# Statistics queued later, the last combinations, a chunk's split and the first stores placed anew in a float32 encoder layer

## The chip, the core and the metric

The kernel runs on one core of one Trainium2 chip. Its time is the device time of one execution in microseconds (us), given as a median of several executions. Beside it stands one profiled execution, from which all durations come. The engines are called as the profile calls them: PE is TensorE (matrix products), PEld its weight loads, DVE is VectorE, ACT is ScalarE, POOL is GpSimd, SP is the engine that issues most transfers. Each takes its instructions in the order in which they were queued.

## The reference, cut to what matters

One layer over 512 tokens of width 2048, all in float32:

```python
xn = rms_norm(x, attn_norm_g)
u_val, u_gate, q, k, v = split(xn @ w_in)
y_conv = conformer_conv(u_val, u_gate, ...)       # GLU, depthwise conv of 31, layer_norm, silu
y_na = neighborhood_attention(q, k, v, rpb)       # 16 heads of 64 on an 8 x 64 grid
mixed = concat([rms_norm(y_conv, conv_out_g), rms_norm(y_na, na_out_g)])
x = x + mixed @ w_out
xn = rms_norm(x, ffn_norm_g)
gate, val = split(depthwise_conv(xn @ w_up, width=3))
x = x + (silu(gate) * val) @ w_down
return rms_norm(x, final_norm_g)
```

`w_up` has 2 x 5632 columns, `w_down` 5632 rows. Every norm needs a sum over all channels of a token before anything can be scaled by it.

## The kernel before, in words

**Layout.** Activations lie with channels on the 128 partitions and the 512 tokens along the free axis. A float32 product is made of three passes in a faster format: weights and activations are split into a high part (rounded, a ScalarE copy, `whi`, line 116) and the rest (a VectorE subtraction, `wlo`, line 117), and `mm3` (lines 127 to 129) adds high x high, high x low and low x high. A unit of weights is 128 x 1024; there are four buffers of each part (`NW`) and seven of raw loads (`NR`), and SP loads a unit when its raw buffer is free.

**Order of work.** The program is written as one stream, and a scheduler orders each engine's queue by priorities (the place in the source, moved by `shifted`) and by what is ready in its own model. Statistics and attention are generators whose steps are queued between the matrix products: `tick` (called when a group of products has been issued) takes the next step from `steps` and from `asteps`. A `yield` in a generator thus means "the rest later, behind the next group of products". A `yield` more or less moves all that follows by one group.

**Statistics of group A.** `group_a` (lines 367 to 396) sums the eight convolution outputs on VectorE (line 373), sums over the partitions by a product with ones (line 376), subtracts the mean, sums the squares (`sum_sq`, line 170), and calls `rsqrt_steps` twice. `rsqrt_steps` sums over partitions to one value per token (line 185), takes the reciprocal root on four values per partition (`root`, lines 173 to 177), spreads it over a diagonal (`dg`, line 197), and yields; its rest multiplies ones with the two diagonals (line 202) and copies the result out (line 206). Both its products use the bank "po" of the pool `psa`. Attention runs beside this: a softmax on VectorE and ScalarE (its last step line 466), transposes on TensorE (line 476), values (line 491), and products that read and write the same pools.

**Output projection and the combinations.** `after` (called for each of 16 blocks d) adds the projection to the residual (line 595), stores it, queues its square for a sum in memory, and on every second block combines two blocks of activations into seven (`b`, `t`, `xc`; lines 609 to 620, `halves` at lines 589 and 590). These seven are the moving side of the up product: the 2 x 2 blocks of weights (A11 to A22) and activations are multiplied with seven products instead of eight. The weights' combinations (lines 650 to 661, on VectorE) are in `factors`.

**The up and down products.** For each of 44 columns f, seven products are made, each over eight k. For the first four columns `up_apart` (line 755) makes them with `mm3`; later `up` (line 669) makes a wide pass (line 700, 512 columns) and a narrow one (line 705, 256 columns). Products use three banks "mm" in turn; the seventh uses "po". ScalarE and VectorE copy and add them out (lines 712 to 751 and 771 to 779), scale by `rstd2` (lines 794, 795), convolve (786 to 788), apply silu (797) and multiply (798). `stats2` loads the sums of squares and makes `rstd2` with `rsqrt_steps`. Four columns f make a chunk; `in_two` splits each column's result (`hh` on ScalarE, line 803, `hl` on VectorE, line 804), and the chunk's down products are issued within the next chunk (`down`, `down_units`).

**The end.** The last chunk's down products are made for 384 tokens (channels on partitions) and 128 tokens (tokens on partitions). `finish` scales a pair of blocks for the 384 tokens, on VectorE, or with ScalarE and GpSimd together for every third pair, and stores it (line 877, `out_T`); `spread` places this between the last products. The 128 tokens are scaled by gains (line 920) and by their own factor (lines 929, 931) and stored in four parts (line 932, `out_N`).

Of the kernel before, what the change touches and what calls it, by code (L numbers as in the profile page):

```python
# [10 lines left out]
F32 = mybir.dt.float32  # L11
# [5 lines left out]
P = 128  # L17
D = 2048
# [33 lines left out]
ORDER = "aavaav" + "aq" * 4 + "qqqq"  # L52
NORM_AT = 4
NG = GW // 8
RA_AFTER = 5

PCOLS = [("g1", KD), ("dww", NC_ * CK), ("dwb", NC_), ("lng", NC_), ("lnb", NC_), ("cog", NC_),
         ("nag", NC_), ("g2", KD), ("fww", 2 * NF * 3), ("fwb", 2 * NF), ("g3", KD)]
# [9 lines left out]
def layer(ctx: ExitStack, tc: tile.TileContext, xT, xG, w_in, w_v, w_out, w_up, w_down, par, tab, g3, out, last_out):  # L68
# [17 lines left out]
    def t2(name, dt=F32):  # L86
        return tp.tile([P, S], dt, tag="t2k", name=name)
# [76 lines left out]
    def sum_sq(acc, src, first, to=slice(0, S)):  # L164
        if first:
            nc.scalar.activation(acc, src, AF.Square)
        else:
            q = t2("sq")[:, to]
            nc.scalar.activation(q, src, AF.Square)
            nc.vector.tensor_add(acc, acc, q)  # L170
# [5 lines left out]
        nc.vector.tensor_mul(y, y, v)  # L176
        nc.vector.scalar_tensor_tensor(y, y, 1.5, r, op0=ALU.add, op1=ALU.mult)

    def rsqrt_steps(acc, n, name, to=slice(0, S), keep=True, by_token=None):

        m = (to.stop - to.start) // P
        ps = psa.tile([P, S], F32, tag="po", name="st")[:, :m]
        v, r, y = (sm.tile([P, S // P], F32, tag="rs" + c, name="rs" + c)[:, :m] for c in "vry")
        for i in range(m):
            nc.tensor.matmul(ps[:, i:i + 1], acc[:, to.start + i * P:to.start + (i + 1) * P], ones[:, 0:1],
                             start=True, stop=True)
        nc.vector.tensor_scalar(v, ps, 1.0 / n, EPS, op0=ALU.mult, op1=ALU.add)
        root(r, y, v)
        if by_token is not None:
            by_token.append(y)  # L190
        yh, yl = (sm.tile([P, S // P], dt, tag="rs" + c, name="rs" + c)[:, :m] for c, dt in (("h", F32R), ("l", F32)))
        nc.vector.tensor_copy(yh, y)
        nc.vector.tensor_sub(yl, y, yh.bitcast(F32))
        ds = []
        for part in (yh.bitcast(F32), yl):
            ds.append(t2("dg", F32R)[:, :m * P])
            nc.vector.tensor_mul(ds[-1].rearrange("p (i k) -> p i k", k=P), ident.unsqueeze(1).broadcast_to([P, m, P]),
                                 part.unsqueeze(2).broadcast_to([P, m, P]))
        yield
        ps = psa.tile([P, S], F32, tag="po", name="st")[:, :m * P]  # L200
        for i, dg in enumerate(ds):
            nc.tensor.matmul(ps, ones_r, dg, start=i == 0, stop=i == 1)
        if not keep:
            return ps
        res = t2(name)
        nc.scalar.activation(res, ps, AF.Copy)
        return res
# [157 lines left out]
    ma, ra = [], []  # L365

    def group_a():
        yield
        yield
        acc = t2("acc")  # L370
        nc.vector.tensor_add(acc, ys[0], ys[1])
        for i in range(2, NC_):
            nc.vector.tensor_add(acc, acc, ys[i])
        yield
        ps = psa.tile([P, S], F32, tag="po", name="st")
        nc.tensor.matmul(ps, ones, acc, start=True, stop=True)
        mu = t2("mu")
        nc.vector.tensor_scalar(mu, ps, 1.0 / CONV, None, op0=ALU.mult)
        acc = t2("acc")
        for i in range(NC_):  # L380
            nc.vector.tensor_sub(ys[i], ys[i], mu)
            sum_sq(acc, ys[i], i == 0)
        yield
        yield
        r = yield from rsqrt_steps(acc, CONV, "rln")
        acc = t2("acc")
        for i in range(NC_):
            nc.vector.tensor_mul(ys[i], ys[i], r)
            nc.scalar.activation(ys[i], ys[i], AF.Silu, scale=pc("lng", i), bias=pc("lnb", i))
            ma.append(split(ys[i], pc("cog", i), "ma"))  # L390
        for i in range(NC_):
            sum_sq(acc, ys[i], i == 0)
        for _ in range(RA_AFTER):
            yield

        ra.append((yield from rsqrt_steps(acc, CONV, "ra")))


# [194 lines left out]
    def after(d, ps):  # L593

        nc.vector.tensor_add(x2[d], x2[d], ps)
        nc.sync.dma_start(xd[d], x2[d])
        q = t2("sq")
        nc.scalar.activation(q, x2[d], AF.Square)

        if d < 2:  # L600
            nc.gpsimd.dma_start(sq2[d], q)
        else:
            nc.gpsimd.dma_start(sq2[d % 2], q, accum_op=ALU.add)
        if d % 2 == 0:
            return
        b = []
        for i in (d - 1, d):
            t = t2("b")
            nc.scalar.activation(t, x2[i], AF.Copy, scale=pc("g2", i))
            b += [t[:, :H], t[:, H:]]  # L610
        b11, b12, b21, b22 = b
        t = t2("t")
        t1, t2_ = t[:, :H], t[:, H:]
        nc.vector.tensor_sub(t1, b11, b12)
        nc.vector.scalar_tensor_tensor(t2_, b22, -1.0, t1, op0=ALU.mult, op1=ALU.subtract)
        t = t2("t")
        t3, t4_ = t[:, :H], t[:, H:]
        nc.vector.tensor_sub(t3, b22, b12)
        nc.vector.scalar_tensor_tensor(t4_, t2_, -1.0, b21, op0=ALU.mult, op1=ALU.subtract)
        for c, f in enumerate((t4_, t1, t3, b11, t2_, b21, b22)):  # L620
            halves(f, c)
# [9 lines left out]
    def stats2():  # L631
        acc2, q = t2("acc2"), t2("sq")
        nc.sync.dma_start(acc2, sq2[0])
        nc.sync.dma_start(q, sq2[1])
        yield
        nc.vector.tensor_add(acc2, acc2, q)
        rstd2.append((yield from rsqrt_steps(acc2, D, "rstd2")))

    def factors(f):

# [113 lines left out]

    def up_apart(f, between):

        def product(c):
            w = weights()
            ps = (psa.tile([P, S], F32, tag="po", name="pu") if c == 6 else
                  psm.tile([P, S], F32, tag="mm", name="pu"))[:, :H]  # L760
            for k in range(U):
                m = comb[c][k]
                i = mm3(ps, w, k, m[:, :H], m[:, H:], k == 0, k == U - 1)
            tick(i)
            between(c)
            return ps

        vv, v, uu, g = (t2(n).rearrange("p (i t) -> p i t", i=2) for n in ("vv", "vl", "uu", "g"))
        both = lambda x: x.unsqueeze(1).broadcast_to([P, 2, H])
        for i in range(2):  # L770
            nc.scalar.activation(vv[:, i], product(i), AF.Copy)
        u, u2 = uu[:, 0], uu[:, 1]
        add(v, vv, both(product(2)))
        nc.scalar.activation(u, product(3), AF.Copy)
        add(u2, u, product(4))
        add(v, v, both(u2))
        add(vv[:, 1], vv[:, 1], u2)
        add(g[:, 0], u, product(5))
        add(g[:, 1], vv[:, 1], product(6))
        return tuple(t.rearrange("p i t -> p (i t)") for t in (g, v))  # L780
# [38 lines left out]
                nc.gpsimd.dma_start(xd[d], t, accum_op=ALU.add)  # L819

    pend = None
    for c in range(NCH):
        hs = []
        for i in range(CH):

            last = c == NCH - 1 and i == CH - 1
            if c and i == CH - 1:
                hs = [in_two(h) for h in hs]
            hs.append(hidden(c * CH + i, lambda at: None if last else down(pend, down_units(c, i, at))))
        hs = [h if isinstance(h, tuple) else in_two(h) for h in hs]  # L830
        if not last:
            pend = hs

# [29 lines left out]

    fm, tm = slice(0, LT), slice(LT, S)

    def finish(pair, r, apart):

        o = t4([P, 2, LT], "fin")
        for i in range(2):
            d = 2 * pair + i  # L870
            x, g = x2[d][:, fm], pc("g3", d)
            if apart:
                nc.scalar.activation(x, x, AF.Copy, scale=g)
                nc.gpsimd.tensor_mul(o[:, i], x, r)
            else:
                nc.vector.scalar_tensor_tensor(o[:, i], x, g, r, op0=ALU.mult, op1=ALU.mult)
        nc.sync.dma_start(out[pair], o)

    acc = t2("acc3")
    for d in range(KD):  # L880
# [13 lines left out]
    def spread(g, k):  # L894
        if (g, k) == (0, 1):
            next(stats)
        elif (g, k) == (1, 1):
            try:
                next(stats)
            except StopIteration as e:  # L900
                rb.append(e.value)
            rb.append(t2("rb")[:, fm])
            nc.scalar.activation(rb[1], rb[0], AF.Copy)
        elif rb and pairs:
            at = pairs.pop(0)
            finish(at, rb[at % 3 == 1], at % 3 == 1)

    for g, ps in enumerate(banks):
# [8 lines left out]
            spread(g, k)  # L917
        nc.scalar.activation(t2("sq"), ps, AF.Square, accum_out=sums[:, g:g + 1])
        xg.append(t2("xg"))
        nc.vector.tensor_mul(xg[g], ps, gains[g])  # L920
        if g == CH - 2:
            nc.vector.tensor_reduce(v, sums[:, :CH - 1], axis=AX.X, op=ALU.add)
            nc.vector.tensor_scalar(v, v, 1.0 / D, EPS, op0=ALU.mult, op1=ALU.add)
# [1 line left out]
    nc.vector.scalar_tensor_tensor(v, sums[:, CH - 1:], 1.0 / D, v, op0=ALU.mult, op1=ALU.add)  # L925
    root(r, y, v)
    for g in range(CH):
        if g % 2:
            nc.scalar.activation(xg[g], xg[g], AF.Copy, scale=y)
        else:  # L930
            nc.vector.tensor_scalar(xg[g], xg[g], y, None, op0=ALU.mult)
        nc.sync.dma_start(last_out[:, g * S:(g + 1) * S], xg[g])
# [74 lines left out]
```

## Time and profile before

| what | value |
|---|---|
| median of 3 runs | 2038.44 us (2037.53 to 2039.32) |
| the profiled execution | 2039.84 us |
| its span, first to last instruction | 2038.1 us |
| mean granted TensorE clock | 0.998 |
| bytes moved | 276.40 MB, mean 136 GB/s |

How to read it: the page gives each engine's busy time, then the chain of work that ended last, then groups of instructions. In a row of the timeline the first number is the start in us, the second the duration, then engine, line, operation, output and inputs, the count, and in brackets how long the engine had been idle and which engine and tile ended that. In the waits, the numbers are total us, times, and the longest. In the windows, each engine has its busy time with the number of instructions, then come the granted TensorE clock, the share of the transfer engines, and GB/s.

### The profile page before, as it was taken

How to read it: one execution, taken by the hardware profiler on the slowest of the kernel's cores; microseconds unless marked ns; L12 is line 12 of the kernel's file. 1: busy time of each engine (PE TensorE's matmuls, PEld its weight loads, DVE VectorE, ACT ScalarE, POOL GpSimd, SP SyncE). 2: the span in 40 equal slices, each digit the busy share in tenths (PEclk: the TensorE clock that was granted, in tenths of full speed). 3: DMA queues.
4: the chain of work that ended last, by engine and by line, in shares of the span. 5: the costliest groups of instructions: out<-in, count | busy, mean ns of one | idle time of the engine just before them, and what ended most of it. 6: DMA issues, size and time to landing. Idle time of an engine off the chain costs nothing.

```text
span 2038.1 us, 28060 instructions
## 1 busy us (share of the span) xinstructions
PE 2021.4 (99%) x10608; PEld 1727.4 (85%) x10608; DVE 1664.6 (82%) x2278; ACT 1036.9 (51%) x1658; POOL 159.7 (8%) x188
## 2 busy tenths in 40 slices
PE   9999999999999999999999999999999999999998
PEld 7888888878888898888888888888888888888887
DVE  7986888878577898888888878888888888889875
ACT  7323234347345555555555555555555555555563
POOL 0000000000001001111111111111111111110111
PEclk9999999999999999999999999999999999999999
DMA  7233333336337445566565565566566566565583
GB/s 255 83 104 90 113 98 104 105 121 212 105 123 179 110 123 137 122 151 145 129 142 145 127 144 142 128 144 145 118 152 145 124 145 145 129 141 124 145 212 120
DMA packets 97063, 276.40 MB, mean 136 GB/s; under 512 B 10912, under 2 KB 11424, under 8 KB 96928
## 3 DMA queue, kind: packets, MB, share of 16 engines
q1 hardware_dynamic: 71568, 228.45, 36.6%
q0 software_dynamic: 25216, 46.15, 15.5%
q8 instruction: 84, 1.38, 0.3%
q14 instruction: 51, 0.42, 0.1%
q10 hardware_dynamic: 144, 0.01, 0.0%
HBM read 220.04 MB, written 54.53 MB: 135 GB/s over the span
## 4 chain that ended last, share of the span: by engine, by line
PE 95%; DVE 2%; ACT 1%; issue 1%; DMA 0%; ACTq 0%; DVEq 0%
PE pu L700 25%; PE pu L705 13%; PE pd L129 8%; PE pd L127 8%; PE pd L128 8%; PE pj L127 5%; PE pj L129 5%; PE pj L128 5%; PE po L127 3%; PE po L129 3%; PE po L128 3%; PE pv L307 1%; PE pv L309 1%; PE pv L308 1%; PE pu L127 1%; PE pu L128 1%
## 5 line engine op out<-in xcount | busy, mean ns | idle before, releaser
L116 ACT ACTIVATE whi<-raw 128x1024 fp32r<-128x1024 f32 x364 | 384.9, 1059 | 504.7 <-PE pj L128 147.7
L117 DVE TENSOR_TENSOR wlo<-raw,whi 128x1024 fp32r<-128x1024 f32 x364 | 443.9, 1220 | 215.4 <-ACT whi L116 205.7
L700 PE MATMUL pu<-xc,whi 128*128 128x512 f32 x2240 | 574.8, 392 | 0.9 <-ACT pl L712 0.9
L700 PEld LDWEIGHTS pu<-xc,whi 128*128 128x128 f32 x2240 | 409.1, 189 | 75.0 <-ACT pl L712 1.2
L705 PEld LDWEIGHTS pu<-xc,wlo 128*128 128x128 f32 x2240 | 305.6, 190 | 21.9
L705 PE MATMUL pu<-xc,wlo 128*128 128x256 f32 x2240 | 312.3, 282 | 0.0
L129 PE MATMUL pd<-hh,wlo 128*128 128x512 f32 x640 | 249.2, 391 | 0.0
L128 PE MATMUL pd<-hl,whi 128*128 128x512 f32 x640 | 249.2, 389 | 0.0
L127 PE MATMUL pd<-hh,whi 128*128 128x512 f32 x640 | 249.0, 391 | 0.0
L819 POOL DMA_DIRECT2D x2d<-pdc x160 | 139.6, 874 | 1167.6 <-ACT pdc L818 1053.8
L128 PE MATMUL pj<-xl,whi 128*128 128x512 f32 x512 | 200.4, 391 | 0.0
L129 PE MATMUL pj<-xh,wlo 128*128 128x512 f32 x512 | 200.2, 391 | 0.0
L127 PE MATMUL pj<-xh,whi 128*128 128x512 f32 x512 | 198.7, 392 | 0.0
L712 ACT ACTIVATE pl<-pu 128x256 f32<-128x256 f32 x280 | 104.4, 382 | 168.3 <-PE pu L700 168.2
L116 ACT ACTIVATE whi<-ws 128x1024 fp32r<-128x1024 f32 x132 | 139.7, 1059 | 76.8 <-PE pu L700 55.2
L361 DVE SCALAR_TENSOR_TENSOR y<-ch,prm,y 128x500 f32<-128x500 f32 (+14 forms) x240 | 173.4, 740 | 4.5
L117 DVE TENSOR_TENSOR wlo<-ws,whi 128x1024 fp32r<-128x1024 f32 x132 | 160.8, 1218 | 19.7 <-ACT whi L116 19.6
L129 PEld LDWEIGHTS pd<-hh,wlo 128*128 128x128 f32 x640 | 120.1, 188 | 28.8 <-DVE wlo L117 3.0
L128 PEld LDWEIGHTS pd<-hl,whi 128*128 128x128 f32 x640 | 120.2, 188 | 25.0
L127 PEld LDWEIGHTS pd<-hh,whi 128*128 128x128 f32 x640 | 120.5, 188 | 21.8
L818 ACT ACTIVATE pdc<-pd 128x512 f32<-128x512 f32 x160 | 93.8, 588 | 84.6 <-PE pd L129 84.5
L127 PEld LDWEIGHTS pj<-xh,whi 128*128 128x128 f32 x512 | 96.4, 188 | 21.3 <-issue 1.9
(197 smaller groups left out, 2851.5 us busy)
## 6 DMA issues: line engine op xcount, KB each, us to landing
raw<-in_w_up SPq DMA_DIRECT2D x176, 512.0 KB, 3.7
raw<-in_w_down SPq DMA_DIRECT2D x88, 512.0 KB, 3.9
x2d<-pdc POOLq DMA_DIRECT2D x160, 256.0 KB, 4.8
raw<-in_w_in SPq DMA_DIRECT2D x60, 512.0 KB, 3.7
raw<-in_w_out SPq DMA_DIRECT2D x32, 512.0 KB, 3.7
raw<-in_w_v SPq DMA_DIRECT2D x16, 512.0 KB, 4.0
tab<-in_tab SPq DMA_DIRECT2D x32, 256.0 KB, 4.9
x<-in_xG SPq DMA_DIRECT2D x16, 256.0 KB, 5.4
```

Of the source, the lines that this page charges most:

```text
L116: i = nc.scalar.activation(hi[:, :n], raw[:, :n], AF.Copy)
L117: j = nc.vector.tensor_sub(lo[:, :n], raw[:, :n], hi[:, :n].bitcast(F32))
L127: nc.tensor.matmul(ps, hi[:, a], mh, start=start, stop=False)
L128: nc.tensor.matmul(ps, hi[:, a], ml, start=False, stop=False)
L129: return nc.tensor.matmul(ps, lo[:, a], mh, start=False, stop=stop)
L307: nc.tensor.matmul(ps, xh, wh[:, f], start=kk == 0, stop=False)
L361: nc.vector.scalar_tensor_tensor(y[:, a:b], h[:, a + j - PAD:b + j - PAD], prm[:, o + j:o + j + 1], y[:, a:b], op0=ALU.mult, op1=ALU.add)
L700: return nc.tensor.matmul(ps, w[0][:, k * P:(k + 1) * P], comb[c][k], start=k == 0, stop=k == U - 1)
L705: nc.tensor.matmul(ps[:, H:], w[1][:, k * P:(k + 1) * P], comb[c][k][:, :H], start=False, stop=False)
L712: nc.scalar.activation(to, ps, AF.Copy)
L818: nc.scalar.activation(t, ps, AF.Copy)
L819: nc.gpsimd.dma_start(xd[d], t, accum_op=ALU.add)
```

## The change

- `group_a`: the two leading yields go; a yield is added after the fourth block of the first loop; the second loop of square sums is merged into the loop before it, with a yield after every second block; `RA_AFTER` is 2 instead of 5.
- `rsqrt_steps` can use the bank "sc" (`free`) and more than one yield before its rest (`rest`); `stats2` uses both, and yields twice more after adding its sums.
- `after`: the combination is a function of its own, and the last one (d = 15) gets a priority higher by 200.
- `up_apart`: for f = 0 the first two products both run to k = 6, then each takes its k = 7.
- The split of the last column of the chunk before the last is made within the last chunk's first column, after its product 3 (`behind`).
- The end: pair 0 is scaled right after the second statistics product, ahead of the copy `rb`, and stored as two transfers; the last of the four parts of the 128 tokens is scaled from its bank in one step, and parts 1 and 2 go to ScalarE.

```diff
-RA_AFTER = 5
+RA_AFTER = 2
...
-    def rsqrt_steps(acc, n, name, to=slice(0, S), keep=True, by_token=None):
+    def rsqrt_steps(acc, n, name, to=slice(0, S), keep=True, by_token=None, free=False, rest=1):
+
+        def bank():
+            if free:
+                return psa.tile([P, 2, S], F32, tag="sc", name="st")[:, 0]
+            return psa.tile([P, S], F32, tag="po", name="st")
...
-        ps = psa.tile([P, S], F32, tag="po", name="st")[:, :m]
+        ps = bank()[:, :m]
...
-        yield
-        ps = psa.tile([P, S], F32, tag="po", name="st")[:, :m * P]
+        for _ in range(rest):
+            yield
+        ps = bank()[:, :m * P]
...
     def group_a():
-        yield
-        yield
         acc = t2("acc")
...
             sum_sq(acc, ys[i], i == 0)
+            if i == NC_ // 2 - 1:
+                yield
         yield
         yield
         r = yield from rsqrt_steps(acc, CONV, "rln")
...
             ma.append(split(ys[i], pc("cog", i), "ma"))
-        for i in range(NC_):
             sum_sq(acc, ys[i], i == 0)
+            if i % 2:
+                yield
         for _ in range(RA_AFTER):
             yield
-
         ra.append((yield from rsqrt_steps(acc, CONV, "ra")))
...
-        if d % 2 == 0:
-            return
+        if d % 2:
+            with shifted(-200 if d == KD - 1 else 0):
+                combine(d)
+
+    def combine(d):
         b = []
...
         nc.vector.tensor_add(acc2, acc2, q)
-        rstd2.append((yield from rsqrt_steps(acc2, D, "rstd2")))
+        yield
+        yield
+        rstd2.append((yield from rsqrt_steps(acc2, D, "rstd2", free=True, rest=2)))
...
+        def first_two():
+            got = [begin(c) for c in range(2)]
+            for c in range(2):
+                tick(part(c, *got[c], range(U - 1)))
+            for c in range(2):
+                part(c, *got[c], range(U - 1, U))
+            return [ps for _, ps in got]
...
-        for i in range(2):
-            nc.scalar.activation(vv[:, i], product(i), AF.Copy)
+        for i, ps in enumerate(first_two() if f == 0 else map(product, range(2))):
+            nc.scalar.activation(vv[:, i], ps, AF.Copy)
...
+    def behind(c, i, at):
+        if c == NCH - 1 and (i, at) == (0, 3):
+            pend[-1] = in_two(pend[-1])
+        down(pend, down_units(c, i, at))
...
-            hs.append(hidden(c * CH + i, lambda at: None if last else down(pend, down_units(c, i, at))))
-        hs = [h if isinstance(h, tuple) else in_two(h) for h in hs]
+            hs.append(hidden(c * CH + i, lambda at: None if last else behind(c, i, at)))
+        if c != NCH - 2:
+            hs = [h if isinstance(h, tuple) else in_two(h) for h in hs]
...
-        nc.sync.dma_start(out[pair], o)
+            if split:
+                nc.sync.dma_start(out[pair][:, i], o[:, i])
+        if not split:
+            nc.sync.dma_start(out[pair], o)
...
+            finish(pairs.pop(0), rb[0], split=True)
             rb.append(t2("rb")[:, fm])
             nc.scalar.activation(rb[1], rb[0], AF.Copy)
...
-        nc.vector.tensor_mul(xg[g], ps, gains[g])
+        if g < CH - 1:
+            nc.vector.tensor_mul(xg[g], ps, gains[g])
...
-        if g % 2:
+        if g == CH - 1:
+            nc.vector.scalar_tensor_tensor(xg[g], banks[g], y, gains[g], op0=ALU.mult, op1=ALU.mult)
+        elif g:
             nc.scalar.activation(xg[g], xg[g], AF.Copy, scale=y)
```

More of the change, by code (lines that the diff above doesn't have):

```diff
@@ L755, in up_apart, with begin, part, product @@
     def up_apart(f, between):
[L757 to L761, printed above, removed]
+        def begin(c):
+            return weights(), (psa.tile([P, S], F32, tag="po", name="pu") if c == 6 else
+                               psm.tile([P, S], F32, tag="mm", name="pu"))[:, :H]
+        def part(c, w, ps, ks):
+            for k in ks:
                 m = comb[c][k]
                 i = mm3(ps, w, k, m[:, :H], m[:, H:], k == 0, k == U - 1)
-            tick(i)
+            return i
+        def product(c):
+            w, ps = begin(c)
+            tick(part(c, w, ps, range(U)))
             between(c)
             return ps
+        def first_two():
[5 more added lines that the diff above has]
+            return [ps for _, ps in got]
         vv, v, uu, g = (t2(n).rearrange("p (i t) -> p i t", i=2) for n in ("vv", "vl", "uu", "g"))
         both = lambda x: x.unsqueeze(1).broadcast_to([P, 2, H])
-        for i in range(2):
-            nc.scalar.activation(vv[:, i], product(i), AF.Copy)
+        for i, ps in enumerate(first_two() if f == 0 else map(product, range(2))):
+            nc.scalar.activation(vv[:, i], ps, AF.Copy)
         u, u2 = uu[:, 0], uu[:, 1]
@@ L864, in layer, with finish @@
     fm, tm = slice(0, LT), slice(LT, S)
-    def finish(pair, r, apart):
+    def finish(pair, r, apart=False, split=False):
         o = t4([P, 2, LT], "fin")
```

## The prediction, as recorded before the run

> **What bounds the kernel now.** I read the page's busy shares and its chain first, then TensorE's waits, then the timeline around each of those waits.
>
> ```profile
> span 2038.1 us, 28060 instructions
> PE 2021.4 (99%) x10608; PEld 1727.4 (85%) x10608; DVE 1664.6 (82%) x2278; ACT 1036.9 (51%) x1658; POOL 159.7 (8%) x188
> PE 95%; DVE 2%; ACT 1%; issue 1%; DMA 0%; ACTq 0%; DVEq 0%
> ```
>
> TensorE is busy for 2021.4 of 2038.1 us, and the chain that ended last is 95% TensorE. The diff removes no matmul. So the change can win only what TensorE idles, 16.7 us, and what it loses to its clock. TensorE's waits are these:
>
> ```profile
> ...
> PE st L376 <- DVE acc L373: 1.3, 1, 1.3
> PE st L202 <- DVE dg L197: 1.1, 1, 1.1
> PE trp L476 <- DVE tab L466: 0.9, 1, 0.9
> PE pu L700 <- ACT pl L712: 0.9, 1, 0.9
> PE pu L127 <- ACT rstd L206: 0.7, 1, 0.7
> PE pu L127 <- ACT xc L589: 0.6, 1, 0.6
> ```
>
> These six are single waits, all at places that the diff touches. The rest of the idle time is the start of the kernel, which the diff leaves alone, and the tail after the last matmul.
>
> A shown wait understates what is lost, as matmuls overlap:
>
> ```profile
> 478.04 0.39 PE L127 MATMUL pj<-xh,whi 128*128 128x512 f32 x1
> 478.26 0.39 PE L128 MATMUL pj<-xl,whi 128*128 128x512 f32 x1
> ...
> 689.62 0.28 PE L128 MATMUL pu<-xc,whi 128*128 128x256 f32 x1
> 689.74 0.28 PE L129 MATMUL pu<-xc,wlo 128*128 128x256 f32 x1
> ```
>
> A 512-wide one lasts 0.39 us and the next starts after 0.22 to 0.23; a 256-wide one lasts 0.28 and the next starts after 0.12. In both cases a wait shown as g costs g + 0.16.
>
> **The change part by part.**
>
> *Statistics of group A* (two yields dropped at the start, one added in the first loop, others moved).
>
> ```profile
> 411.54 0.69 DVE L410 TENSOR_TENSOR q<-pj,rstd 128x512 f32<-128x512 f32 x1 [5.29 <-PE pj L129]
> 416.87 0.66 PE L491 MATMUL po<-pt,vg 128*64 128x128 f32 x8
> 431.86 1.41 DVE L373 TENSOR_TENSOR acc<-acc,y 128x512 f32<-128x512 f32 x2
> 433.41 1.10 PE L376 MATMUL st<-acc,ones 128*128 128x512 f32 x2 [1.32 <-DVE acc L373]
> 471.28 3.07 DVE L170 TENSOR_TENSOR acc<-acc,sq 128x512 f32<-128x512 f32 x4
> 479.56 0.63 PE L476 MATMUL trp<-ident,tab 128*128 128x128 f32 x4 [0.91 <-DVE tab L466]
> ```
>
> L376 waits because its seven sums (0.7 us each, 1.41 for two) were mixed with an attention's softmax. In the changed program L376 stands 20 matmuls ahead of the values at 416.87, so at about 412.3, and its sums fall into VectorE's idle 5.29 us from 406.2: 7 x 0.7 = 4.9, done at 411.2. The wait goes with 1.1 us to spare: 1.32 + 0.16 = 1.48. The 1.10 of L376 itself stays. The second wait, of the transposes, comes from the run of square sums (four in 3.07 at 471.28), which held back the softmax. The sums now lie between the activations in the loop, and the transposes get some 5 us of slack: 0.91 + 0.16 = 1.07. What is late next: the four column sums of the variance (L185), behind eight subtractions, squares and sums. Carried on by these rows, VectorE ends them within 0.1 us of L185's new slot, near 432.7. I take 0.25 for that tie, with bounds of 0 and 0.7 (one sum). The earlier table loads pass only weight loads with slack on SP; with them, the queue costs nothing. Part A: -1.48 - 1.07 + 0.25 = **-2.30**.
>
> *Last combination, first two products.*
>
> ```profile
> 679.59 0.39 PE L127 MATMUL pu<-xc,whi 128*128 128x256 f32 x1 [0.62 <-ACT xc L589]
> ```
>
> The diff puts the last k of the first two products behind both products and gives the last combination a higher priority. In the built orders nothing of it arrives: before, too, both products run to k = 6 before either takes k = 7; and VectorE still has the weight combination L652, which waits for its load, ahead of the combination's L614. This wait stays: 0.
>
> *The second statistics (L185, L202, L206).*
>
> ```profile
> 685.57 0.99 PE L185 MATMUL st<-ones,acc 128*128 128x1 f32 x8
> 690.00 1.06 ACT L116 ACTIVATE whi<-ws 128x1024 fp32r<-128x1024 f32 x1 [1.78 <-PE pu L128]
> 690.32 0.68 DVE L197 TENSOR_TENSOR dg<-ident,rsh 128x512 fp32r<-128x512 f32 x1
> 691.15 1.01 PE L202 MATMUL st<-dg,ones 128*128 128x512 f32 x2 [1.13 <-DVE dg L197]
> 692.85 0.39 PE L127 MATMUL pu<-xc,whi 128*128 128x256 f32 x1 [0.69 <-ACT rstd L206]
> 693.50:696.90 3.40, 3.40 (x18) 3.40 (x17) 2.84 (x5) 0.00 (x0) 0.00 (x0) 0.50 0.00 0
> 693.55 0.41 PE L127 MATMUL pu<-xc,whi 128*128 128x256 f32 x1
> ...
> 696.54 0.41 PE L129 MATMUL pu<-xc,wlo 128*128 128x256 f32 x1
> 698.44 1.22 DVE L650 TENSOR_TENSOR ws<-raw 128x1024 f32<-128x1024 f32 x1
> ```
>
> What is lost before: 1.13 + 0.16 ahead of L202; 1.01 - (0.23 + 0.39) = 0.39 between its two matmuls, the second of which waits for the second dg; 0.69 + 0.16 behind it, as product 6 shares the bank "po" with the statistics. That is 2.53. Then the clock: right behind these waits the granted clock is 0.50 for 3.4 us (column 0.50 of the window's row), and 15 matmuls start 2.99/14 = 0.214 apart instead of 0.12; for 16 of them that is 16 x 0.094 = 1.5. In all 4.03.
>
> After: L185 stands behind the first matmul of product 4 (about 686.2) and finds its sum ready (VectorE, by the same rows, at 686.0). L202 goes to bank "sc" and to the place behind product 6, so product 6 needs no copy: the wait for L206 goes. L202's slot is 686.17 + 0.85 (L185, less its overlap with the next) + 71 x 0.12, near 695.5. But its dg now has three long steps ahead on VectorE, in this order: the split wlo of the weights that take over product 5's buffer, L650, then dg. The whi that feeds this split waits for the last L128 of product 5 (692.42). As at 690.00, it starts 0.38 behind that L128's start and takes 1.06: 693.86. The split, by L117's 1.22 of which 0.08 overlaps the next: 695.0; two 128x4 steps and L650 (1.22): 696.3; dg (0.68): 697.0, and L202 starts 0.15 behind it, as at 691.15 after 690.32 + 0.68: 697.15. So L202 waits **1.6** in its new place. The second dg is 0.6 later, which three matmuls of the next product cover. That product's bank needs ScalarE's copy L774 behind a whi, done near 697.0: covered by the same wait. Bounds of the new wait: 0.4 if VectorE reaches dg ahead of L650, 2.8 if one more 1.22 step slips in; I keep the worked 1.6. The clock: 1.6 in one stretch against 1.13 + 0.39 + 0.69 within 3 us before; L376's 1.32 alone brought no drop. I take full clock. Part B: -4.03 + 1.6 = **-2.43**.
>
> The Trainium skill, "TensorE: Matmul & The Clock Gate", Part 1 (HAM clock gate), says the clock halves after an idle window of about 3.4 us and that gaps under about 3 us are safe. Here the half clock lasts about such a window (3.4), yet no wait near it is above 1.13, so the trace disagrees with the bound on gaps; by that rule the 1.5 would not hang on these waits.
>
> *Last chunk's split (`behind`).*
>
> ```profile
> 1866.37 0.63 ACT L803 ACTIVATE hh<-uy 128x512 fp32r<-128x512 f32 x1 [0.76 <-DVE uy L798]
> 1866.91 0.36 ACT L712 ACTIVATE vv<-pu 128x256 f32<-128x256 f32 x1
> 1867.18 0.38 ACT L712 ACTIVATE pl<-pu 128x256 f32<-128x256 f32 x1
> 1867.60 1.88 PE L700 MATMUL pu<-xc,whi 128*128 128x512 f32 x7 [0.90 <-ACT pl L712]
> ```
>
> The product at 1867.60 needs the bank that the copy at 1867.18 frees; that copy stood behind hh, which waited for VectorE. In the changed order both copies stand right behind their product, which ends two products (8 x 0.23 + 8 x 0.12 = 2.8 each) before the third one's end at 1866.7, so near 1861.1; and hh follows the third product. Its reader, the down product, comes only after product 3 of the second block, over 20 us later. Moving two copies up (0.27 from one to the next) delays the whi behind them by 0.55, which its weights' lead of more than one product covers. Part C: -(0.90 + 0.16) = **-1.06**.
>
> *The end.*
>
> ```profile
> DMA  0000001000000299999999999999999991000000
> GB/s 0 0 0 0 0 0 30 0 0 0 0 0 0 112 385 391 402 397 408 386 402 385 413 391 397 402 386 413 367 372 384 387 384 63 0 0 0 0 0 0
> 2022.12 0.49 ACT L903 ACTIVATE rb<-st 128x384 f32<-128x384 f32 x1 [2.64 <-PE st L202]
> 2022.65 3.76 DVE L876 SCALAR_TENSOR_TENSOR fin<-x,prm,st 128x384 f32<-128x384 f32 x7 [1.57 <-ACT rb L903]
> 2024.65 2.00 POOL L874 TENSOR_TENSOR fin<-x,rb 128x384 f32<-128x384 f32 x2
> 2024.72 6.27 SPq L877 DMA_DIRECT2D out_T<-fin  x8
> ```
>
> From 2018 in slices of 0.55 us, the engines move about 390 GB/s without a hole from 2025.6 to 2036.4: 8 x 393 + 4 x 262 kB = 4.2 MB. So the end is set by when that flow starts, not by VectorE or ScalarE. Today SP's first store is GpSimd's pair (done 2024.65). After, pair 0 leaves as two stores from 2022.8 (0.39 MB, before the flow); but the copy rb, which GpSimd needs, now waits for VectorE's first two fin (0.54 each by 3.76 for seven, 1.15 with the hand-over), so GpSimd's pair is done at 2025.8, and SP, in order, holds the rest behind it. 3.8 MB from 2026.75 (0.9 behind the issue, as now) at 390 GB/s: 9.75, to 2036.5. VectorE's chain gets shorter by an L920 but ends nothing. Bounds -0.5 and +0.5: **0**.
>
> Sum: -2.30 - 2.43 - 1.06 = **-5.8**. Against the profiled execution (2038.1 + 1.7 around it = 2039.8) that is 2034.0; the median of the runs is 2038.44, 1.4 below that execution, so the forecast for a median is **2032.6**.
>
> **The rivals.**
> - *Half clock stays* (1.5 less): the 1.6 us wait in the new place brings it as the old ones did, or, as the skill's rule would have it, it never hung on them. For: 1.6 is longer than any single wait near 693. Against: total idle there falls from 2.2 to 1.6. 2038.44 - 4.3 = 2034.1.
> - *No wait in the new place*: VectorE gets to dg in time. Against: the in-order chain above. 2038.44 - 7.4 = 2031.0.
> - *Part A doesn't do what it says*: the chain of the variance moves with the sums, and L185 or the transposes take over the wait; of 2.55 nothing remains. For: the tie. 2032.6 + 2.3 = 2034.9.
> - *Slower*: L650, ahead of dg, waits for a weight load that SP issues only when the wlo of product 6 is done (near 689.6). It has 5.4 us, against a median of 3.7 to landing in the page's row:
>
> ```profile
> raw<-in_w_up SPq DMA_DIRECT2D x176, 512.0 KB, 3.7
> ```
>
>   Every microsecond beyond costs TensorE one, with a half-clock stretch of 1.5 on top. 5.8 - 1.5 = 4.3 beyond, so a landing 9.7 us after issue, is where this turns slower; at 14 us it gives 2038.44 + 4.3 = 2042.7. Against: three loads would have to share the engines, whose rate there is low.
>
> **How the numbers follow.** Chances: forecast 0.50 (own range 2031.4 to 2034.0), half clock 0.25, no wait 0.08, part A 0.12, slower 0.05. About 0.2% (4.1 us, 2034.4) is what a measurement of this kernel can tell from no change. The forecast lies under that line nearly whole, half clock straddles it, part A is above it: faster 0.62, same 0.33, slower 0.05. The range takes forecast, no wait, half clock and most of part A, with the ties' bounds: 2030.8 to 2036.2.
>
> **What would show it.** In the profile after: no wait at L376, at L476 or at L700; 0.6 still at L127 for xc; one wait of about 1.4 shown at L202 for dg, none for rstd; granted clock 1.00 between 690 and 705; the flow of the stores ending about 8 us behind the last matmul, with a hole after pair 0. A larger wait at L185, or a half clock behind L202, would make the forecast wrong.

## The result, and the profile after

The changed kernel takes **2034.74 us** (median of 21 executions, 2033.82 to 2035.87) against 2038.44 us (21 executions, 2037.53 to 2040.66). The ratio is 0.998 with a 95% interval of 0.9974 to 0.9986, so 2.9 to 5.3 us less; by the medians it is 3.70 us. The forecast was 2032.6, with a range of 2030.8 to 2036.2. In the two profiled executions the difference is larger: 2039.84 to 2034.68 us. The gap between these two differences is the subject of most of what follows. (The function `up` begins at line 692, not 669.)

The page of the changed kernel, its first lines:

```profile
span 2032.9 us, 28056 instructions
PE 2019.5 (99%) x10608; PEld 1726.0 (85%) x10608; DVE 1664.4 (82%) x2277; ACT 1036.5 (51%) x1658; POOL 159.7 (8%) x188
```

TensorE's waits in the changed kernel (its lines have moved: L208 and L202 are before's L202 and L197, L595 is before's L589):

```profile
PE idle L237 <- DVE warm L234: 1.6, 1, 1.6
PE st L208 <- DVE dg L202: 1.5, 1, 1.5
PE pu L127 <- ACT xc L595: 0.7, 1, 0.7
```

Of the six waits that the prediction listed, four are gone (L376, the transposes, the copy at L700, rstd), the one for xc is still there, and the one for dg has moved and grown. TensorE's timeline around it, then VectorE's:

```profile
693.75 0.28 PE L129 MATMUL pu<-xc,wlo 128*128 128x256 f32 x1
695.48 0.47 PE L208 MATMUL st<-dg,ones 128*128 128x512 f32 x1 [1.45 <-DVE dg L202]
695.79 0.28 PE L127 MATMUL pu<-xc,whi 128*128 128x256 f32 x1
```

```profile
692.22 1.23 DVE L117 TENSOR_TENSOR wlo<-raw,whi 128x1024 fp32r<-128x1024 f32 x1 [0.32 <-ACT whi L116]
...
693.44 1.22 DVE L661 TENSOR_TENSOR ws<-raw 128x1024 f32<-128x1024 f32 x1
...
694.65 0.69 DVE L202 TENSOR_TENSOR dg<-ident,rsh 128x512 fp32r<-128x512 f32 x1
```

The wait shown is 1.45, so 1.45 + 0.16 = 1.61 is lost; 1.6 was forecast, by the same queue: a split that waits for its whi, the sum at L661 (before's L650), then dg. Between 690 and 705 the clock stays at full speed.

The end of the changed kernel, from 2013 on in slices of 0.55 us:

```profile
DMA  0000010002960006999999999999999990000000
GB/s 0 0 0 0 0 30 0 0 0 101 366 249 0 0 0 263 413 374 419 380 419 380 408 397 391 408 374 402 380 391 365 391 354 4 0 0 0 0 0 0
```

Pair 0 leaves early, then three slices are empty, and the flow runs to the end. From the end of the last matmul to the end of the span it is 9.52 us (2023.39 to 2032.91), against 9.38 before.

### The profile page after: what moved, and what is told of

It is laid out like the page before. It is cut to its first block, busy times and chain, and to the rows that moved or that the text cites. A ratio compares the mean times of both kernels' runs of the same rounds, so it can differ in the third digit from the quotient of the medians.

```text
span 2032.9 us, 28056 instructions
## 1 busy us (share of the span) xinstructions
PE 2019.5 (99%) x10608; PEld 1726.0 (85%) x10608; DVE 1664.4 (82%) x2277; ACT 1036.5 (51%) x1658; POOL 159.7 (8%) x188
## 4 chain that ended last, share of the span: by engine, by line
PE 98%; DVE 1%; issue 0%; ACT 0%; DMA 0%; ACTq 0%; DVEq 0%
PE pu L711 25%; PE pu L716 13%; PE pd L129 8%; PE pd L127 8%; PE pd L128 8%; PE pj L127 6%; PE pj L129 6%; PE pj L128 6%; PE po L127 3%; PE po L129 3%; PE po L128 3%; PE pv L314 1%; PE pv L313 1%; PE pv L315 1%; PE pu L127 1%; PE pu L128 1%
## 5 line engine op out<-in xcount | busy, mean ns | idle before, releaser
L711 PE MATMUL pu<-xc,whi 128*128 128x512 f32 x2240 | 574.5, 391 | 0.0
L711 PEld LDWEIGHTS pu<-xc,whi 128*128 128x128 f32 x2240 | 409.1, 189 | 73.8
```

The source lines that it names most:

```text
L711: return nc.tensor.matmul(ps, w[0][:, k * P:(k + 1) * P], comb[c][k], start=k == 0, stop=k == U - 1)
```

## The experiments

**Theory 1**, formed from the result: the terms of the sum are right, but two of them (the half clock behind the second statistics, and 0.7 of the 1.06 at the copy) belonged to the one profiled execution and not to one at the median. **Theory 2**: the half clock follows those waits in every execution, and something else in the changed kernel costs 1.5 to 2 us.

### The kernel before, four more profiles

`base1`, `base2`, `base3`, `base4`: no edit.

> The kernel before once more, for a second look at its clock. Theory 1 (the half clock behind the second statistics is in some executions only, and the typical one is without it): the granted clock around 693 may be 1.00, and then the span is 1.5 us under the first profile's 2038.1, near 2036.6, with all six waits as they were. Theory 2 (the half clock follows those waits in every execution): 0.50 for 3.4 us again, span 2038.1 within 0.4.

> A third look at the kernel before, same expectations as the second: theory 1, span near 2036.6 where the clock stays at 1.00, or 2038.1 where it is halved; theory 2, 2038.1 and 0.50 each time.

> The kernel before, fourth profile. Theory 1: of its executions about half have the half clock (times fell into two groups, 2036.2 to 2037.1 and 2037.6 to 2038.6 us of span); where the span is under 2037.2 the clock between 690 and 700 is 1.00 although the waits for dg (1.1) and rstd (0.7) are there. Theory 2: 0.50 for 3.4 us whatever the span.

> The kernel before, fifth profile, same as the fourth: by theory 1 the clock between 690 and 700 is 1.00 where the span is under 2037.2, and halved where it is over 2037.6; by theory 2 it is halved whatever the span.

Measured: spans of 2038.0, 2038.5, 2036.6 and 2037.5 us. In each, TensorE waits 1.3 for acc, 1.1 for dg, 0.9 for the transposes' table and 0.7 for rstd, as in the first profile. The clock is halved in `base1` and `base2` and stays full in `base3` and `base4`. The trace's clock record changes only in steps of 3.413 us from where the clock first rose (at 7.44 in the first profile, 8.14, 7.99, 6.81, 6.87 in the other four), so the stretch just ahead of each possible change can be cut out. Windows of the first profile, of `base1`, `base3` and `base4`, in this order (us of the window, PE busy with the count, then the other engines; PEclk is the third number from the end):

```profile
690.11:693.52 3.41, 1.64 (x7) 1.05 (x8) 3.38 (x7) 1.82 (x3) 0.00 (x0) 1.00 0.28 107
693.52:696.93 3.41, 3.41 (x18) 3.41 (x17) 2.82 (x5) 0.00 (x0) 0.00 (x0) 0.50 0.00 0
```

```profile
690.80:694.22 3.42, 1.94 (x10) 1.35 (x11) 3.42 (x6) 1.52 (x3) 0.00 (x0) 1.00 0.23 90
694.22:697.63 3.41, 3.41 (x19) 3.41 (x18) 2.52 (x4) 0.00 (x0) 0.00 (x0) 0.50 0.00 0
```

```profile
689.47:692.88 3.41, 2.18 (x13) 1.38 (x11) 3.27 (x9) 1.06 (x2) 0.00 (x0) 1.00 0.66 251
692.88:696.29 3.41, 2.76 (x23) 2.77 (x24) 3.41 (x6) 0.87 (x2) 0.00 (x0) 1.00 0.00 0
```

```profile
689.53:692.94 3.41, 2.23 (x14) 1.52 (x12) 3.27 (x9) 1.06 (x1) 0.00 (x0) 1.00 0.70 258
692.94:696.36 3.42, 2.73 (x23) 2.65 (x23) 3.42 (x6) 0.87 (x2) 0.00 (x0) 1.00 0.02 5
```

The same waits were split over two windows in `base3` and `base4`, which left TensorE busy for 2.18 and 2.23 of 3.41 us; in the first profile and in `base1` they fell into one, which left 1.64 and 1.94 (1.55 in `base2`), and the next window ran at half. Theory 2 falls: same kernel, same waits, no half clock. The spans of 21 more executions of before, which ran beside the last eight experiments, lie from 2036.2 to 2038.7 and fill the range, and `base4`, with a full clock, lies between the two groups that were expected. So the half clock is not the only thing that varies.

Another is the last chunk's copy. VectorE's step L652 in the first profile, in `base3` and in `base4`:

```profile
1859.59 1.23 DVE L652 TENSOR_TENSOR raw<-raw 128x1024 f32<-128x1024 f32 x1 [1.53 <-DMA raw<-in_w_up]
```

```profile
1858.11 1.23 DVE L652 TENSOR_TENSOR raw<-raw 128x1024 f32<-128x1024 f32 x1 [0.78 <-DMA raw<-in_w_up]
```

```profile
1859.00 1.23 DVE L652 TENSOR_TENSOR raw<-raw 128x1024 f32<-128x1024 f32 x1 [1.50 <-DMA raw<-in_w_up]
```

VectorE waits there for a weight load, and everything behind it up to hh is late by as much. Where that wait is 1.5, TensorE's at L700 is 0.9 (the first profile and `base4`). Where it is 0.8 to 0.9, TensorE's is 0.2 or 0.3, or too small to be listed (`base1`, `base2`, `base3`). The loss at L700 is thus 1.06, 0.36, 0.44, 0.31 and 1.04 in the five profiles.

Compared matmul by matmul, the other four profiles drift away from `base3` at three places, and by 0.16 at most anywhere else: in the first 25 us, while the first activations are loaded (0.45 ahead to 0.34 behind), at the half clock (1.47 to 1.49 where it occurs), and at this copy (0.04 to 0.75).

Three of five profiles have the half clock, so it is not rare. That the median of the first 21 executions lacks both losses is inferred: its span, near 2036.7 (the time less the 1.8 around it, an estimate from the profiled executions), is that of `base3`; the three with the half clock are 1.4 to 1.9 longer. It also depends on the set of executions: the two later sets of before, 12 and 9 executions, have medians of 2039.43 and 2039.66, 1.0 and 1.2 above the first. Why the sets differ was not traced.

### Without the middle part, and the middle part alone

`act`: the changes of `group_a`, `RA_AFTER`, `behind` and the end; the rest as before. `b_all`: the changes of `rsqrt_steps`, `stats2`, `combine` and `first_two`; the rest as before. Two of the hunks, the first in `b_all` only, the second in `act` only:

```diff
-        rstd2.append((yield from rsqrt_steps(acc2, D, "rstd2")))
+        yield
+        yield
+        rstd2.append((yield from rsqrt_steps(acc2, D, "rstd2", free=True, rest=2)))
```

```diff
-RA_AFTER = 5
+RA_AFTER = 2
```

> Only group A's statistics, the late split and the end are changed; the second statistics stay as before. Both theories: no wait at L376, at the transposes, at L700; the waits for dg (1.1) and for rstd (0.7) stay, and so does 0.6 to 0.7 for xc. Matmuls end 2.2 + 1.1 = 3.3 us earlier than in an execution of before with the same clock. Theory 2: clock 0.50 for 3.4 us behind these waits, span near 2034.9. Theory 1: either that, or clock 1.00 and 2033.4.

> Only the second statistics, the last combination's priority and the two interleaved products are changed. Both theories: the waits at L376, the transposes and L700 stay; one wait of 1.4 to 1.5 for dg, none for rstd, clock 1.00 between 690 and 705; xc's wait stays at 0.6 to 0.7. Against an execution of before with half clock 2.4 us less (2035.7), against one without it 0.9 less. So theory 2 has its time 2.4 under the kernel before run beside it, theory 1 mostly 0.9.

Measured: `act` has a span of 2034.0 us and a clock of 1.00 in that place; `b_all` 2035.9, against 2036.4 of the kernel before beside them. Waits of `act`, then of `b_all`:

```profile
PE st L202 <- DVE dg L197: 1.1, 1, 1.1
PE pu L127 <- ACT rstd L206: 0.7, 1, 0.7
PE pu L127 <- ACT xc L589: 0.5, 1, 0.5
```

```profile
PE st L208 <- DVE dg L202: 1.5, 1, 1.5
PE st L382 <- DVE acc L379: 1.3, 1, 1.3
PE trp L482 <- DVE tab L472: 0.9, 1, 0.9
PE pu L127 <- ACT xc L595: 0.6, 1, 0.6
PE pu L711 <- ACT pl L723: 0.3, 1, 0.3
```

Each half removes its own waits and no other (the 0.3 at L711 in `b_all` is the copy with its load on time); `act` is one more case in which the waits for dg and rstd bring no half clock, since they fall into two windows (busy 2.42 and 2.53 of 3.41). The 2034.0 of `act` is 0.6 above the 2033.4 of theory 1, as this execution was 0.70 behind the first profile already after the first 25 us. `b_all` is 0.5 under the kernel before beside it, nearer to theory 1's 0.9 than to theory 2's 2.4. One execution each has a spread of over 1 us at this size, so this pair says more by its waits than by its times.

### The wait for dg

`d_dg`: the changed kernel, with one weight sum of column 2 (the one at L661 above) behind the second dg. The rest of the edit only keeps hold of the two dg instructions.

```diff
             a["s"] = t4([P, U * P], "ws")
-            add(a["s"], load(A21), a[A22])
+            load(A21)
+            with tc.issue_after(dgs[1].ins) if f == 2 else nullcontext():
+                add(a["s"], a[A21], a[A22])
```

> The changed kernel, with VectorE's weight sum (before's L650) of column 2 queued behind the two dg instead of ahead of them. Theory (TensorE's new wait of 1.45 at the second statistics is VectorE's queue): dg is written 1.1 us earlier, the wait falls to about 0.3, but then the second of the two products waits 0.36 for the second dg and the next product near 0.3 for ScalarE's copy of its bank, so matmuls end 0.6 to 0.8 earlier than in the changed kernel (2023.4 becomes 2022.6 to 2022.8). Rival (dg waits for the split fed by product 5 alone): wait and end stay within 0.2.

Measured: 2033.94 us; matmuls end at 2022.57 instead of 2023.39.

```profile
PE idle L238 <- DVE warm L235: 1.6, 1, 1.6
PE pu L127 <- ACT xc L596: 0.5, 1, 0.5
PE st L209 <- DVE dg L203: 0.5, 1, 0.5
```

The wait falls from 1.45 to 0.45. It was VectorE's queue, not the split alone. But that the end, 0.82 earlier, is close to what was expected is luck. Compared matmul by matmul with the changed kernel's profile, this execution was 0.43 ahead before the edited place, from its first 25 us, and 0.18 more at xc. The edit won 0.57 at dg, and 0.45 was given back between 764 and 773, where the first down products begin. So it is worth about 0.1.

### The wait for xc

`d_xc`: the changed kernel, with the weight combination of column 1 behind the last step of the last combination of activations (`done`, kept by the rest of the edit).

```diff
+            elif c == 2 and f == 1:
+                load(A11)
+                with tc.issue_after(done[0].ins):
+                    add(a[A21], a[A21], a[A11])
+                return a[A21]
             elif c == 2:
```

> The changed kernel, with the weight combination (before's L652) of column 1 queued behind the last activation combination. Theory (TensorE's wait for xc, 0.5 to 0.8, is this one VectorE step of 1.14 ahead of the combination): the wait goes or falls under 0.1, matmuls end 0.7 to 0.9 earlier. Rival (ScalarE's copies b and xc set it, as the interleaved order could not remove it): at least 0.3 of it stays. The wait for dg may change by up to 0.8, since the steps on VectorE are shifted.

Measured: 2033.50 us; matmuls end at 2022.18, 1.2 earlier.

```profile
PE idle L237 <- DVE warm L234: 1.6, 1, 1.6
PE st L208 <- DVE dg L202: 1.2, 1, 1.2
```

The wait for xc is gone (0.96 won there, matmul by matmul), and the wait for dg is 0.28 shorter. So the diff's interleaving and its priority aimed at a real wait and missed its cause: one step of 1.2 us that the scheduler had put ahead.

### The order of the stores

Both on the changed kernel; `d_pairs` has the first edit, `d_pairs2` both:

```diff
-    pairs = list(range(KD // 2))
+    pairs = [0, 2, 1, 3, 4, 5, 6, 7]
...
-            nc.sync.dma_start(out[pair], o)
+            with tc.issue_after(stores[0].ins) if pair == 1 else nullcontext():
+                stores.append(nc.sync.dma_start(out[pair], o))
```

> The changed kernel, with the pairs finished in the order 0, 2, 1, 3 to 7, so that SP's third store is one of VectorE and GpSimd's comes fourth. Theory (the flow of stores starts late because SP stands behind GpSimd's pair): the flow after the hole starts 0.9 earlier and the tail from the last matmul to the end falls from 9.5 to between 8.6 and 9.0. Rival (the last four stores, which wait for the tokens' own factor, set the end): tail 9.3 to 9.6.

> The order that the run before it was meant to have: pair 2's store is now really queued ahead of GpSimd's pair. Theory (the flow starts late because SP stands behind GpSimd's pair): SP's third store is issued near 0.9 earlier, the flow after the hole starts that much earlier, and the tail from the last matmul to the end falls from 9.5 to between 8.6 and 9.1. Rival (the last four stores set the end): the flow starts earlier and gets a second hole ahead of them, tail 9.3 to 9.6.

Measured: `d_pairs` 2035.02 us with a tail of 9.47. It did not do what it was made for: the scheduler still put GpSimd's store first, so it tells nothing of the theory. `d_pairs2` has the order that was meant: 2033.55 us, tail 8.60. Stores of `d_pairs` and of `d_pairs2`, and the flow of `d_pairs2` from 2012:

```profile
2017.72 0.87 SPq L909 DMA_DIRECT2D out_T<-fin  x2
2020.84 5.27 SPq L911 DMA_DIRECT2D out_T<-fin  x7
```

```profile
2017.17 0.87 SPq L909 DMA_DIRECT2D out_T<-fin  x2
2019.39 5.27 SPq L912 DMA_DIRECT2D out_T<-fin  x7
2025.95 2.07 SPq L971 DMA_DIRECT2D out_N<-xg  x4
```

```profile
GB/s 0 0 0 0 0 0 0 30 0 0 20 352 341 3 39 380 408 391 386 402 391 413 374 419 385 408 385 372 387 387 391 372 220 0 0 0 0 0 0 0
```

The third store comes 2.2 us behind the first instead of 3.1, the hole shrinks to one or two slices, and the tail falls by 0.9. The end is set by when the flow starts, as the prediction had it; and SP's wait behind GpSimd's pair was the 0.9.

### The edits together

`d_best` joins `d_dg`, `d_xc` and `d_pairs`; `d_best2` joins `d_dg`, `d_xc` and `d_pairs2`.

> The three edits together. If each does what its theory says: 0.7 + 0.8 + 0.6 = 2.1 us under the changed kernel's median, so near 2032.6, and 5.8 under the kernel before. By the three rivals: within 0.5 of the changed kernel. The runs of the kernel before beside it show its spans: by theory 1 two groups, near 2036.4 and near 2038.

> The three working edits: VectorE's sum behind dg, its combination behind xc, and the store of pair 2 ahead of GpSimd's. Two of them together gave 2033.66, 1.1 under the changed kernel; with 0.6 for the stores 2033.1. If the last four stores set the end, 2033.7.

Measured: `d_best` 2033.66 us (8 executions, 2033.24 to 2033.94); `d_best2` **2032.71 us** (6 executions, 2032.43 to 2033.55), a ratio to the kernel before of 0.9967 (0.9955 to 0.998). Against the changed kernel's median that is 1.1 and 2.0 less, where the first expected 2.1 and the second 1.6. The changed kernel ran in the first set, though, and before was slower beside these two: against it they are 5.8 and 7.0 less, where the changed kernel was 3.7 less. What the edits add is thus known only as 1.1 to 2.1 and 2.0 to 3.3. With `d_pairs` empty, 1.5 was left for `d_best`; up to 695.9 it is 1.62 ahead of the changed kernel, and 0.6 of it is given back between 760 and 775, where the first down products begin. Waits of `d_best2`:

```profile
PE idle L238 <- DVE warm L235: 1.6, 1, 1.6
PE st L209 <- DVE dg L203: 0.4, 1, 0.4
PE pd L128 <- DVE hl L837: 0.2, 1, 0.2
```

The last row shows a part of it: the sum that was moved makes VectorE late for the split hl. The rest of the 0.6 was not traced. All three profiles with the moved sum give back 0.45 to 0.7 there, about what they won at dg (0.57), and `d_xc`, `d_pairs` and `d_pairs2` give back nothing. So two of the three edits work: the one for xc and the order of the stores.

## Why the prediction was right or wrong, step by step

| step | forecast | measured |
|---|---|---|
| group A's statistics | -2.30 | -1.48 - 1.07 + 0.19 = -2.36 (by the starts of the matmuls ahead of and behind it, -2.2) |
| last combination, first two products | 0 | 0.78 lost before, 0.86 after: 0 within the spread (0.69 to 0.98 in eleven profiles) |
| second statistics, waits | -2.53 + 1.6 = -0.93 | -2.53 + 1.61 = -0.92 |
| second statistics, clock | -1.5 | -1.5 in three profiles of before, 0 in two |
| last chunk's split | -1.06 | -1.06 and -1.04 in two profiles of before, -0.31 to -0.44 in three |
| the end | 0 | +0.14 |

The mechanisms held, each at its place. Group A: the sums fell into VectorE's idle stretch, the transposes got their slack, and the tie at L185 cost 0.19 (0.25 was taken). The interleaving changed nothing, as the built orders said. The new wait for dg came at the forecast place, from the forecast queue, at the forecast size. At the end, the flow of the stores decided, with the hole behind pair 0 that was forecast.

The median, 2034.74, lies in the range of 2030.8 to 2036.2, but above the 2031.4 to 2034.0 that the forecast case gave itself. The 3.70 is also under the 4.1 that the prediction set as the line between same and faster: what came is the "same" that it gave 0.33, not the "faster" that it gave 0.62.

**The steps that were off are two sizes.** The first is in "for 16 of them that is 16 x 0.094 = 1.5. In all 4.03.": this term was taken as part of the median. It is the price of a coincidence: those waits fall into one window of 3.41 us in some executions and into two in others. The second is "Part C: -(0.90 + 0.16)": the 0.90 was VectorE late by one weight load of that execution, and is 0.2 to 0.3 where the load is on time. Without the clock, and with 0.37 for the copy (mean of the three profiles), the sum is -2.36 - 0.92 - 0.37 + 0.14 = -3.5, and the medians gave -3.70. With both in, it is -5.7, and the two profiled executions gave -5.2; of that difference +0.35 arose in the first 16 us, while the first activations are loaded, and 0.2 in group A. That -3.5 and -3.70 agree so well is in part luck, since the interval is 2.9 to 5.3 and the median of before moves by 1.0 to 1.2 between sets. `d_pairs`, which is the changed kernel but for an order that did not take effect, was 4.4 below before in its set (one execution).

There was a sign of it in the numbers at hand: the profiled execution was 1.4 above the median of its own kernel. The prediction named this, and then subtracted the profile's whole sum from the median. An execution that is 1.4 slow has 1.4 of losses, on balance, that one at the median lacks, and the change can't win those from the median.

Of the rivals, "Part A doesn't do what it says" gave 2034.9 and came nearest, by luck: part A won what was forecast. "Half clock stays" gave 2034.1, and the term that it drops is one of the two that were missing, but for another reason than it stated: not that the new wait brings the half clock back, but that executions at the median, by their span, never had it. Whether the new wait sometimes brings it is open: in the changed kernel's profile the window with the wait, 693.73 to 697.14, has TensorE busy for 1.96 of 3.41, next to the 1.94 at which `base1` was halved, and two of its 21 executions are 0.8 and 1.1 above the median.

The Trainium skill, "TensorE: Matmul & The Clock Gate", Part 1, says that the window is free-running, so that the same kernel has a different number of slow matmuls at its start from run to run. The five profiles of before show the like in mid-kernel (half from 693.52, 694.22 and 694.07, or not at all). The bound that the prediction took from the same page, no idle gaps above about 3 us (it stands in the section "Why this matters for your kernels"), does not hold here: the longest single wait in a window that was followed by the half clock was 1.14.

## What to carry to other kernels

Before a profile's losses are subtracted from a median, ask which of them the median has: an execution that is 1.4 us above the median has losses of its own, and a second and third profile of the kernel before would have shown both here. Short waits close together are worth removing or spreading even when each is small, since the half clock followed here on how busy TensorE was in a window of 3.41 us, not on one long gap. Where a scheduler orders the queues, look in the built order for the one step that stands ahead of the late one; moving that step removed the 0.86 lost there, where a priority and an interleaving of the consumers removed nothing. And judge an edit matmul by matmul against a second trace, ahead of the edited place, at it and behind it: the end of `d_dg` looked like the forecast, and the edit was worth 0.1.

## What the runs showed of the hardware that was not expected

In mid-kernel the clock was halved for exactly one window of 3.41 us, after windows in which TensorE's records were busy for 1.55, 1.64 and 1.94 us of 3.41, and not after windows with 1.96, 2.18, 2.23, 2.42 and 2.53. Windows of the changed kernel at the wait for dg and at the kernel's end, then one of the first profile at the wait for acc:

```profile
693.73:697.14 3.41, 1.96 (x15) 1.70 (x14) 3.41 (x6) 1.90 (x3) 0.00 (x0) 1.00 0.44 154
...
2021.50:2024.91 3.41, 1.89 (x9) 1.22 (x7) 3.03 (x8) 1.22 (x5) 2.96 (x4) 1.00 1.02 397
2024.91:2028.32 3.41, 0.00 (x0) 0.00 (x0) 1.79 (x6) 1.33 (x3) 0.00 (x0) 1.00 1.02 397
2028.32:2031.70 3.38, 0.00 (x0) 0.00 (x0) 0.00 (x0) 0.00 (x0) 0.00 (x0) 0.50 0.84 314
```

```profile
430.69:434.10 3.41, 2.09 (x10) 1.31 (x8) 3.38 (x6) 1.06 (x1) 0.00 (x0) 1.00 0.52 154
```

So there is no sharp line in these numbers. With all fourteen profiles cut in this way, the clock fell after every window with 1.64 or less, and after none with 1.96 or more. In between it went both ways: it fell after the 1.94 of `base1`, and stayed full after 1.77, 1.88 and 1.89, the windows with the last matmuls of `d_pairs2`, `d_xc` and the changed kernel. The ends of matmuls are modelled in the trace, so what the clock goes by is not shown more closely than "about half of a window". The same waits for dg and rstd cost 1.5 us or nothing, by where they fall: the wait for dg ended 0.75 to 1.34 us into the window in the three profiles that were halved, and 0.15, 2.35 and 2.49 us into one in `act`, `base3` and `base4`, which were not.
